# Moving two loads in a one-layer encoder kernel: the second gate weight tile in front of the first attention loads, and the attention mask into the opening

## The chip, the cores and the metric

The kernel runs on one NeuronCore of one Trainium2 chip. The metric is the device time of one execution in microseconds (us), lower is better. TensorE (PE in the profile, with its weight loads as PEld) does matrix products, VectorE (DVE) and ScalarE (ACT) do elementwise work, GpSimd (POOL) does a little arithmetic and issues DMAs, SyncE (SP) only issues DMAs. Each engine runs its own instructions in order; SP and POOL are also queues in which a DMA that has to wait holds up the DMAs behind it.

## The reference

One layer of a streaming encoder, for a prompt of 1024 tokens and a sample of 32 tokens with 512 cached ones, width 1024, all in float32. What matters here:

```python
ada = silu(c) @ w_ada + b_ada                      # six modulation vectors
h   = rms_norm(x, g_pre_mix) * (1 + sc1) + sh1
p   = h @ w_in                                     # columns: q latent 384 | kv latent 256 | rope key 32
                                                   #          | SB q 512 | SB k 512 | SB v 512 | gate A 1024 | gate B 1024
...
# branch B, stick-breaking attention, strictly causal
z    = (q_b @ k_b.T) * SB_SCALE
mask = kpos[None, :] < qpos[:, None]
sp   = where(mask, softplus(z), 0);  later = reverse_cumsum(sp) - sp
o_b  = where(mask, exp(log_sigmoid(z) - later), 0) @ v_b
...
merged = sigmoid(g_a) * (o_a @ w_proj_a) + sigmoid(g_b) * (o_b @ w_proj_b)
x = x + gt1 * rms_norm(merged @ w_out, g_post_mix)
# then a convolutional FFN and its residual
```

## The kernel before, in words

The stages run one after the other in one program: the opening (`stage_h`: modulation and the normed, transposed input), the projections to SB queries, keys and values (`stage_qkv`), stick-breaking attention (`stage_sb`), latent attention, merge, and the FFN. Products are made to float32 precision from a high and a low part of each operand: a raw weight tile of 128 x 1024 floats is loaded into a buffer `wr`, ACT writes its rounded high part `wh` (helper `hi`, L68) and DVE the rest `wl` (helper `lo`, L71), and three matmuls are accumulated (L75 to L77). There are two buffers each of `wr`, `wh` and `wl`.

**Opening.** `stage_h` loads four tiles of the prompt, the weights of the first half of the modulation (`ada_half(0)`), normalizes and transposes, loads the first `w_in` tiles, then the other four tiles and the second half.

**Projections.** `stage_qkv` makes most of the products two weight tiles at a time in `pair()` (five pairs; the last is q 2 and q 3). Each product has two column blocks `b`, and its banks in PSUM are copied out by ACT between products (L611, L619, L627, L636). Behind pair number 3 (the fourth) stands the load of the mask of the sample's attention, `k_mask[:, 128:]`, 128 x 272 floats, into a buffer `sg` by POOL, and its copy by ACT to `msk` in bfloat16 (L687, L688). `msk` is read much later, in `sb_sample` (stage_lat). After the last pair, gate tile 0 (columns 2208 to 2335 of `w_in`) is loaded and split.

**Stick-breaking.** `stage_sb` first loads queries, keys and values of head 0 (`queries(0, 0)`, six loads, and `values(0, 0)`), which the projections have spilled to DRAM. From then on every load of this stage goes through `load` (L83) with `issue_after(self.sent)`, so that SP issues them in the order in which they are written. Inside the stage the order on PE, ACT and DVE is written out by hand as a string `ORDER`, in which each letter is a step and what follows is the head's group, row block and half:

```python
S0.0 a0.0 f1 S0.1 f1 a0.1 e0.0 S1.0 f1 l0.0 f1 e0.1 f1 a1.0 l0.1 e1.0 f1 x0.0 c0.0 f1 d0.0 E0.0 f2 S2.0a
x0.1 c0.1 f1 l1.0 f1 a2.0a x1.0 d0.1 c1.0 W f1 e2.0a f1 G l2.0a w x2.0a f1 S1.1 f1 a1.1 f1 E0.1 f2 e1.1
```

`S` are scores (L1207, L1208: the second uses the keys' low part `KLz`, loaded from `kl`), `a e l x c d E` the elementwise chain on ACT and DVE (L747 to L767), `T h v V` turn the weights and multiply them by the values. The rest fills PE: `f` is one of the 24 steps (three blocks of 352 tokens, eight steps each) of the product of a gate tile, `G` copies a finished block from PSUM (ACT, L1129) and stores it, `W` and `w` split the next gate tile (ACT, DVE). The generator `gates` (L1096 on) makes these steps; at the first `f` of gate tile m it also loads the raw tile m + 1. Gate tile 1 is therefore written, and issued on SP, behind `queries(0, 0)` and `values(0, 0)`.

Outside such hand-ordered blocks the order on each engine is chosen at compile time by a scheduler with a cost model of its own, so a line can run well before or after its neighbours in the text. Pools of successive stages share memory (`reuse_waits="tile"`): a load into a new tile waits until the last reader of the old tiles under it has run.

Of the kernel before, what the change touches and what calls it, by code (L numbers as in the profile page):

```python
# [44 lines left out]
class K:  # L45
# [329 lines left out]
    def stage_h(self):  # L375
        nc = self.nc
        self.new_H()
        a = self.a
        self.Fq = self.tc.alloc_tile_pool(name="fq", bufs=1, reuse_waits="tile")
        self.fq = self.Fq.tile([P, KT, TP - 512 + TS], F32, name="fq")  # L380
        with self.tc.tile_pool(name="st_h", bufs=2, reuse_waits="tile") as tp, self.tc.tile_pool(name="wada", bufs=8, reuse_waits="tile") as wp:
            self.ada_prep(tp)
            xts = []

            def load(t):
                x = self.tl(wp, [P, D], F32, "x")
                nc.sync.dma_start(x, a["x_prompt"][0, t * P : (t + 1) * P])
                nc.vector.tensor_scalar(x, x, self.rstd(self.sumsq(x, P, tp, "jk0", 1024), D, P), None, ALU.mult)
                xts.append(x)

            def norm(t, hf):
                self.norm_T(t, xts[t : t + 4] if t < 8 else [xs], self.g1, 0, tp, 4 * hf, 4 * hf + 4)

            for t in range(4):
                load(t)
            self.ada_half(0, wp, tp)
            norm(0, 0)
            w = [self.w_in_tile(672)]
            for t in range(4, 8):
                load(t)  # L400
            w.append(self.w_in_tile(672 + 512))
            self.in_w = w
            norm(4, 0)
            xs = self.tl(tp, [P, 256], F32, "xs")
            self.quarters(xs, a["x_sample"][0], nc.gpsimd)
            nc.gpsimd.dma_start(self.sel, a["k_sel"])
            self.ada_half(1, wp, tp)
            nc.vector.tensor_scalar(xs, xs, self.rstd_s(xs, tp), None, ALU.mult)
            norm(0, 1)
            norm(8, 0)  # L410
            norm(4, 1)
            norm(8, 1)
# [30 lines left out]
    def stage_qkv(self):  # L443
# [232 lines left out]
        for i, (ta, tb) in enumerate(pairs):  # L676
            pair(i, ta, tb, *U[i % 2 * 2 : i % 2 * 2 + 2])
            if i == 0:
                with self.tc.issue_after(l2):
                    self.ada_bias(2)  # L680
            elif i == 1:
                late = self.late_loads(sg().bitcast(F32))
            elif i == 2:
                self.late_vectors(late)
            elif i == 3:
                mk = sg().bitcast(F32)[:, :272]
                nc.gpsimd.dma_start(mk, a["k_mask"][:, P:])  # L687
                nc.scalar.copy(self.msk, mk)  # L688
        self.in_w.append(self.w_in_tile(2208))
        for r, c in self.SB:  # L690
            nc.gpsimd.dma_start(self.sbd[r, c], self.sb[r, c])
# [357 lines left out]
    def sb_sample(self, b):  # L1049
# [43 lines left out]
            nc.gpsimd.dma_start(self.obd[k][:, TP:T], os[:, k])  # L1093
        yield

    def gates(self):  # L1096

        nc = self.nc
        v = lambda t: t.rearrange("p (k c) -> p k c", k=8)
        w, ps, ada = [self.w_in_tile(2208)], [], []  # L1100
        self.next_w = w
        raw = []

        def steps():
            for m in range(16):
                wh, wl = w.pop(0)
                for b, (c0, n) in enumerate(self.BLK):
                    if b == 0:
                        c = 2208 + (m + 1) * P if m < 15 else 3 * P
                        raw.append(self.wload([(0, 1024, self.a["w_in"][0, :, c : c + P].rearrange("(k p) c -> p k c", p=P), 8)]))  # L1110
                    ps.append((m, c0, n, self.bank("mm")))
                    for k in range(KT):
                        self.mm3(ps[-1][3][:, :n], wh[:, k], wl[:, k], self.Hh[k][:, c0 : c0 + n],
                                 self.Hl[k][:, c0 : c0 + n], k == 0, k == KT - 1)
                        if k < KT - 1:
                            yield
                    if b == 1 and self.ada_sum is not None:
                        ada.append(self.ada_turn())
                    yield

        step = steps()

        def do(kind):
            if kind == "f":
                next(step)
            elif kind == "G":
                m, c0, n, x = ps.pop(0)
                g = self.tl(self.At, [P, 512], F32, "nat", 3 if self.At is self.Sp else 2)
                nc.scalar.copy(g[:, :n], x[:, :n])  # L1129
                self.gsent = nc.gpsimd.dma_start(self.gd[m, :, c0 : c0 + n], g[:, :n]).ins  # L1130
            elif kind == "A":
                self.ada_step(4, self.sm2, self.Sp, ada)
                if not self.ada_todo:
                    self.sample_load(1)
            elif kind in "DQ":
                ada.pop(0)()
            elif kind == "W":
                w.append((self.tl(self.W, [P, 1024], F32R, "wh"), self.tl(self.W, [P, 1024], F32R, "wl")))
                self.hi(w[0][0], raw[0])
            else:  # L1140
                self.lo(w[0][1], raw.pop(0), w[0][0])
                w[0] = tuple(v(x) for x in w[0])

        return do
# [14 lines left out]
    def stage_sb(self):  # L1159
        nc = self.nc  # L1160
        self.att_rows()
        S = self.Sp = self.At = self.tc.alloc_tile_pool(name="sb", bufs=2, side="right", reuse_waits="tile")
        def place(*tags):
            for g, w, n in tags:
                for _ in range(n):
                    self.tl(S, [P, w], F32R if g[0] == "P" else F32, g, n)

        place(("o", 256, 2), ("PTh", 512, 2), ("PTl", 512, 2))
        self.KLz, Q, KH, V = [None] * 2, [None] * 2, [None] * 2, [None] * 2
        t = lambda n: self.tl(S, [P, TP], F32R, n, 1)  # L1170

        def values(p, h):
            if p:
                V[h] = t(f"V{h}")
            self.load(V[h].bitcast(F32).rearrange("r (t d) -> r t d", t=8), self.vd[p][:, :, h])

        def queries(p, h):
            r, o = slice(64 * h, 64 * h + 64), slice(64 - 64 * h, 128 - 64 * h)
            d = lambda x, n: self.load(x.bitcast(F32), self.spilt[n][p][r])
            if p:  # L1180
                Q[h], KH[h] = t(f"Q{h}"), t(f"KH{h}")
            d(Q[h][r], "qh")
            d(KH[h][r], "kh")
            d(KH[h][o], "kh")
            d(Q[h][o], "ql")
            d(self.KLz[h][r], "kl")
            d(self.KLz[h][o], "kl")

        V[1], self.KLz[1], Q[1], KH[1] = t("V1"), t("KL1"), t("Q1"), t("KH1")
        place(("ada", 256, 2), ("nat", 512, 3))  # L1190
        self.diagonals(S)
        for _ in range(3):
            self.tl(S, [P, TP], F32, "A")
        V[0], self.KLz[0], Q[0], KH[0] = t("V0"), t("KL0"), t("Q0"), t("KH0")
        self.sm2 = self.tc.alloc_tile_pool(name="att", bufs=2, reuse_waits="tile")
        for g, w, n in (("big", BIG, 3), ("A", TP, 2)):
            for _ in range(n):
                self.tl(self.sm2, [P, w], F32, g)

        self.sent = self.wlast  # L1200
        queries(0, 0)
        self.ada_w, self.ada_sum = [], None
        values(0, 0)

        def score(h, ps, i, c0, n):
            q = slice(i * P, (i + 1) * P)
            nc.tensor.matmul(ps[:, :n], Q[h][:, q], KH[h][:, c0 : c0 + n], start=True, stop=False)  # L1207
            nc.tensor.matmul(ps[:, :n], Q[h][:, q], self.KLz[h][:, c0 : c0 + n], start=False, stop=True)  # L1208

        fill = self.gates()  # L1210
        E = mybir.EngineType
        for p in range(4):
            then = {"S2.0a": lambda: queries(p, 1), "S2.1a": lambda: values(p, 1)}
            if p == 0:
                then["S2.1a"] = lambda: (values(p, 1), self.ada_fetch(4, self.sm2))
            if p < 3:
                then.update({"S3.1b": lambda: queries(p + 1, 0), "V3.0": lambda: values(p + 1, 0)})
            with self.tc.manual_schedule(engines={E.PE, E.Activation, E.DVE}):
                self.sb_attend(score, lambda b, h: V[h][:, b * P : b * P + P], self.store(self.obd[p]), fill, then)
        self.in_w.append(self.next_w.pop(0))  # L1220
        S.release()
        self.At = self.sm2
        self.sm3 = self.tc.alloc_tile_pool(name="att2", bufs=2, reuse_waits="tile")
# [1526 lines left out]
```

## Time and profile before

| | |
|---|---|
| median of 3 runs | 1679.88 us (1679.72 to 1681.83) |
| the profiled execution, its own time | 1686.64 us |
| its span, first to last instruction | 1684.8 us |
| PE busy | 98% |
| DVE, ACT, POOL busy | 75%, 60%, 18% |
| mean granted PE clock | 0.992 |
| DMA | 260.62 MB, mean 155 GB/s |

The profiled execution is 0.4% longer than the median of the runs. "Busy" is the share of the span in which an engine executes; a view of waits gives, for an engine and line, the line that ended its idle time, with the sum, the count and the longest. The granted clock is the share of full speed at which PE was allowed to run.

### The profile page before, as it was taken

The page shows a single profiled execution, that of the slowest core. Times are in us where ns is not written, and L with a number is a line of the kernel's source. Part 1 is how long each engine was busy: PE and PEld are TensorE (multiplying, and loading weights), DVE is VectorE, ACT ScalarE, POOL GpSimd, SP SyncE. Part 2 cuts the span into 40 slices and gives each one's busy share as a digit, 9 for nine tenths or more (in the row PEclk, how much of TensorE's full clock was granted, in tenths as well). Part 3 has the DMA queues.
Part 4 walks back from the last instruction along what each step waited for, and adds up shares of the span by engine and source line. Part 5 has one row for each costly group of instructions (what it writes and reads, how often), then busy time and mean ns, then how long its engine had stood idle before and what let it go on. Part 6 is the DMA issues. An engine that isn't in the chain of part 4 may idle for free. (4 is left out here: it accounts for less than half of the span.)

```text
span 1684.8 us, 30265 instructions
## 1 busy us (share of the span) xinstructions
PE 1643.0 (98%) x11592; PEld 1509.2 (90%) x11592; DVE 1268.4 (75%) x2139; ACT 1008.5 (60%) x1946; POOL 300.9 (18%) x581
## 2 busy tenths in 40 slices
PE   6999999999999999999999999999999999999996
PEld 3999999999999889988988799999999999877885
DVE  4865598989883588987766789878778778787455
ACT  4544587878884488987772675544444444454442
POOL 2113312111121221111000222211112111200013
PEclk8999999999999999999999999999999999999999
DMA  9345876566733443231374523333333333797643
GB/s 331 101 130 183 273 226 182 165 169 176 208 109 89 131 103 115 74 97 49 134 266 135 175 89 125 130 126 104 128 126 100 133 128 104 245 331 246 190 142 118
DMA packets 194145, 260.62 MB, mean 155 GB/s; under 512 B 23374, under 2 KB 132304, under 8 KB 193936
## 3 DMA queue, kind: packets, MB, share of 16 engines
q1 hardware_dynamic: 172944, 198.50, 38.0%
q0 software_dynamic: 20688, 59.56, 10.1%
q8 instruction: 91, 1.49, 0.4%
q10 hardware_dynamic: 368, 0.63, 0.1%
q14 instruction: 54, 0.44, 0.1%
HBM read 191.11 MB, written 67.82 MB: 154 GB/s over the span
## 5 line engine op out<-in xcount | busy, mean ns | idle before, releaser
L68 ACT ACTIVATE wh<-wr 128x1024 fp32r<-128x1024 f32 (+2 forms) x151 | 130.1, 863 | 226.8 <-PE s L2204 85.8
L71 DVE TENSOR_TENSOR wl<-wr,wh 128x1024 fp32r<-128x1024 f32 (+2 forms) x151 | 148.2, 984 | 87.1 <-ACT wh L68 86.9
L75 PE MATMUL mm<-hh,wh 128*128 128x352 f32 x456 | 153.4, 336 | 2.8 <-ACT nat L1129 2.8
L76 PE MATMUL mm<-hl,wh 128*128 128x352 f32 x456 | 149.5, 328 | 0.4 <-DVE hl L333 0.4
L77 PE MATMUL mm<-hh,wl 128*128 128x352 f32 x456 | 149.0, 327 | 0.0
L2203 PE MATMUL mm<-T,wh 128*128 128x256 f32 (+1 forms) x376 | 108.2, 288 | 2.0 <-ACT q L627 2.0
L2205 PE MATMUL mm<-T,wl 128*128 128x256 f32 (+1 forms) x376 | 107.1, 285 | 0.4 <-DVE wl L71 0.2
L2204 PE MATMUL mm<-T,wh 128*128 128x256 f32 (+1 forms) x376 | 106.6, 284 | 0.0
L2205 PE MATMUL s<-T,wl 128*128 128x256 f32 (+1 forms) x348 | 99.3, 285 | 0.0
L2203 PE MATMUL s<-T,wh 128*128 128x256 f32 (+1 forms) x348 | 99.2, 285 | 0.0
L2204 PE MATMUL s<-T,wh 128*128 128x256 f32 (+1 forms) x348 | 98.8, 284 | 0.0
L71 DVE TENSOR_TENSOR wl<-S,wh 128x1024 fp32r<-128x1024 f32 (+1 forms) x55 | 59.2, 1077 | 51.7 <-ACT wh L68 51.3
L75 PEld LDWEIGHTS mm<-hh,wh 128*128 128x128 f32 x456 | 86.9, 191 | 6.4 <-ACT nat L1129 3.1
L76 PEld LDWEIGHTS mm<-hl,wh 128*128 128x128 f32 x456 | 87.1, 191 | 3.4 <-DVE hl L333 1.7
L2344 DVE SCALAR_TENSOR_TENSOR u<-u,c,u 128x1058 f32<-128x1058 f32 x68 | 87.0, 1317 | 2.0 <-ACT u L2341 0.7
L808 PE MATMUL tr<-c,A 128*128 128x128 f32 x576 | 87.1, 272 | 0.0
L77 PEld LDWEIGHTS mm<-hh,wl 128*128 128x128 f32 x456 | 86.9, 191 | 0.2
L68 ACT ACTIVATE wh<-S 128x1024 fp32r<-128x1024 f32 (+1 forms) x55 | 51.8, 943 | 47.6 <-PE s L2204 13.4
L2205 PE MATMUL tr<-T,wl 128*128 128x272 f32 (+1 forms) x272 | 77.7, 286 | 0.2 <-DVE wl L71 0.2
L2203 PE MATMUL tr<-T,wh 128*128 128x272 f32 (+1 forms) x272 | 77.8, 286 | 0.0
L2204 PE MATMUL tr<-T,wh 128*128 128x272 f32 (+1 forms) x272 | 77.3, 284 | 0.0
L2334 POOL COPY c<-u 128x2 f32<-128x2 f32 x44 | 26.7, 607 | 265.3 <-DVE u L2280 229.4
(770 smaller groups left out, 5836.8 us busy)
## 6 DMA issues: line engine op xcount, KB each, us to landing
wr<-in_w_up_dram SPq DMA_DIRECT2D x44, 512.0 KB, 4.1
dr<-in_w_down_dram SPq DMA_DIRECT2D x43, 512.0 KB, 5.3
wr<-in_w_in_dram SPq DMA_DIRECT2D x33, 512.0 KB, 6.7
A<-in_w_ada_dram SPq DMA_DIRECT2D x32, 512.0 KB, 5.8
wr<-gdn SPq DMA_DIRECT2D x30, 512.0 KB, 4.2
gdn<-u POOLq DMA_DIRECT2D x23, 512.0 KB, 5.2
gd<-nat POOLq DMA_DIRECT2D x48, 176.0 KB, 3.5
t<-gd SPq DMA_DIRECT2D x16, 528.0 KB, 4.7
```

What stands on the lines that cost most here:

```text
L68: self.nc.scalar.activation(out, in_, AF.Identity, scale=scale)
L71: return self.nc.vector.tensor_tensor(out, full, hi.bitcast(F32), ALU.subtract)
L75: m(ps, lh, rh, start=start, stop=False)
L76: m(ps, lh, rl, start=False, stop=False)
L77: self.pe = m(ps, ll, rh, start=False, stop=stop).ins
L808: self.nc.tensor.transpose(tr[:, (2 * s + q) * P : (2 * s + q + 1) * P], at[q][:, b * P : b * P + P], self.idt)
L2203: m(ps[:, :n], w[0][:, k], x[0][:, k, c], start=first and k == 0, stop=False, skip_group_check=True)
L2204: m(ps[:, :n], w[0][:, k], x[1][:, k, c], start=False, stop=False, skip_group_check=True)
L2205: i = m(ps[:, :n], w[1][:, k], x[0][:, k, c], start=False, stop=k == 3, skip_group_check=True)
L2334: nc.gpsimd.tensor_copy(self.CV[:, 0:2, cc], u[:, 1024:1026])
L2344: nc.vector.scalar_tensor_tensor(y, u[:, w : w + YW], self.cvT[:, w, cc : cc + 1], y, ALU.mult, ALU.add)
```

## The change

Gate tile 1 is no longer loaded by the first `f` step but by `stage_sb` itself, directly in front of `queries(0, 0)`; the other gate tiles are loaded where they were. The mask is loaded in `stage_h` into a small tile of its own, between the first `w_in` tile and the other half of the prompt, again by a DMA of POOL, and turned to bfloat16 by DVE instead of ACT.

```diff
@@ stage_h
             norm(0, 0)
             w = [self.w_in_tile(672)]
+            mk = self.tl(tp, [P, 272], F32, "mk")
+            nc.gpsimd.dma_start(mk, a["k_mask"][:, P:])
+            nc.vector.tensor_copy(self.msk, mk)
             for t in range(4, 8):
                 load(t)
@@ stage_qkv
                 self.late_vectors(late)
-            elif i == 3:
-                mk = sg().bitcast(F32)[:, :272]
-                nc.gpsimd.dma_start(mk, a["k_mask"][:, P:])
-                nc.scalar.copy(self.msk, mk)
         self.in_w.append(self.w_in_tile(2208))
@@ gates
+    def gate_raw(self, m):
+        c = 2208 + m * P if m < 16 else 3 * P
+        return self.wload([(0, 1024, self.a["w_in"][0, :, c : c + P].rearrange("(k p) c -> p k c", p=P), 8)])
+
     def gates(self):
...
-        raw = []
+        raw = [self.ahead]
...
                     if b == 0:
-                        c = 2208 + (m + 1) * P if m < 15 else 3 * P
-                        raw.append(self.wload([(0, 1024, self.a["w_in"][0, :, c : c + P].rearrange("(k p) c -> p k c", p=P), 8)]))
+                        if m:
+                            raw.append(self.gate_raw(m + 1))
@@ stage_sb
+        self.ahead = self.gate_raw(1)
         self.sent = self.wlast
         queries(0, 0)
```

## The prediction

> **What bounds the kernel now.** I read the page first, for the engine that sets the pace.
>
> ```profile
> PE 1643.0 (98%) x11592; PEld 1509.2 (90%) x11592; DVE 1268.4 (75%) x2139; ACT 1008.5 (60%) x1946; POOL 300.9 (18%) x581
> ```
>
> TensorE (PE) is busy in 98% of the span, so an edit elsewhere gains only where it closes a hole in PE or keeps PE's clock up. The second view is the list of waits, for PE alone, from 150 to 400 us, the stretch that holds both edited places; this is its whole answer:
>
> ```profile
> PE mm L75 <- ACT nat L1129: 2.8, 1, 2.8
> PE mm L2203 <- ACT q L627: 2.0, 1, 2.0
> ```
>
> Two holes, 2.8 and 2.0 us, both ended by ScalarE (ACT). The third view is ACT's timeline at both places (start, duration, engine and line; in brackets the idle time before it and what ended that):
>
> ```profile
> 161.57 0.37 ACT L627 COPY q<-mm 128x256 f32<-128x256 f32 x1 [1.16 <-PE mm L2205]
> 165.63 0.42 ACT L688 CAST c<-sg 128x272 bf16<-128x272 f32 x1 [3.69 <-DMA sg<-in_k_mask_dram]
> 165.96 0.62 ACT L68 ACTIVATE wh<-wr 128x512 fp32r<-128x512 f32 x1
> 166.49 0.37 ACT L627 COPY q<-mm 128x272 f32<-128x272 f32 x1
> ...
> 200.06 0.44 ACT L747 ACTIVATE A<-s 128x320 f32<-128x320 f32 x1 [0.88 <-PE s L1208]
> 204.89 1.06 ACT L68 ACTIVATE wh<-wr 128x1024 fp32r<-128x1024 f32 x1 [4.39 <-DMA wr<-in_w_in_dram]
> 205.85 0.45 ACT L749 ACTIVATE A<-A 128x320 f32<-128x320 f32 x1
> 206.21 0.43 ACT L1129 COPY nat<-mm 128x352 f32<-128x352 f32 x1
> ```
>
> At 161.94 ACT stops for 3.69 us at the mask's copy, whose load has not landed; queued behind it is the copy of a PSUM bank that PE must overwrite next. At 200.50 it stops for 4.39 us at the split of gate tile 1 (step W), whose raw tile has not landed; behind it is the evacuation (step G) of the bank that the third block of gate tile 0 needs. The change moves exactly these two loads. PE's timeline and the 2-us windows (busy PE, weight loads, DVE, ACT, POOL, then granted PE clock, DMA share, GB/s) show what each hole costs:
>
> ```profile
> 164.61 0.28 PE L2205 MATMUL mm<-T,wl 128*128 128x256 f32 x1
> 166.91 0.40 PE L2203 MATMUL mm<-T,wh 128*128 128x272 f32 x1 [2.02 <-ACT q L627]
> ...
> 203.39 0.33 PE L76 MATMUL mm<-hl,wh 128*128 128x352 f32 x1
> 203.55 0.32 PE L77 MATMUL mm<-hh,wl 128*128 128x352 f32 x1
> 206.69 0.66 PE L75 MATMUL mm<-hh,wh 128*128 128x352 f32 x1 [2.82 <-ACT nat L1129]
> 209.50 0.47 PE L1207 MATMUL s<-KH,Q 128*128 128x320 f32 x1
> ```
>
> ```profile
> 166.00:168.00 2.00, 1.09 (x8) 1.09 (x9) 1.39 (x3) 2.00 (x6) 0.37 (x1) 1.00 0.00 0
> 206.00:208.00 2.00, 1.31 (x4) 1.31 (x5) 2.00 (x4) 2.00 (x6) 0.57 (x1) 0.62 0.96 313
> 208.00:210.00 2.00, 2.00 (x9) 1.99 (x9) 1.75 (x5) 1.29 (x3) 0.38 (x1) 0.53 0.84 300
> ```
>
> The first hole leaves the clock at 1.00. After the second it is 0.62 and 0.53 for two windows, so that hole costs more than its length.
>
> **Part 1, the mask leaves the projections.** ACT no longer waits at 161.94, and L627 can follow as soon as its product is done, some 3 us earlier than 166.49. PE's 2.02 us come back: **-2.0**. Nothing else is late there: PE has no other wait in this stretch, by the list above. The load's issue on GpSimd's queue (POOL) goes too, and nobody waited for that queue.
>
> **Part 2, gate tile 1 in front.** SyncE's queue (SP) now, the landing of this tile (min/median/max of the one load), and the split of the buffer that it is loaded into:
>
> ```profile
> 181.28 0.54 SPq L83 DMA_DIRECT2D Q<-qh  x1
> 183.95 1.57 SPq L83 DMA_DIRECT2D KL<-kl  x2
> 185.63 1.14 SPq L83 DMA_DIRECT2D V<-vd  x1
> 186.87 1.94 SPq L83 DMA_DIRECT2D wr<-in_w_in_dram  x1
> ...
> DMA to landing us min/median/max: 18.0/18.0/18.0
> ...
> 178.60 1.29 DVE L71 TENSOR_TENSOR wl<-wr,wh 128x512 fp32r<-128x512 f32 x2
> ...
> wr<-in_w_in_dram SPq DMA_DIRECT2D x1, 512.0 KB, 3.8
> ```
>
> Now the tile is issued at 186.87, behind six loads of queries and keys and one of values, and lands 18.0 us later, at 204.9: ACT's wait. There are two raw buffers; the one it gets is last read by the splits that end at 178.60 + 1.29 = 179.89. In front, it can be issued there, and SP is free again before 181.28, when the queries' own buffers become free, so their issue is not delayed. Landing: an equal tile, issued near 175 on quiet queues, took 3.8 us (the last row); at twice that it is there by 188, 12 us ahead of step W. Then W (1.06) and L749 (0.45) run from 200.50 and G near 201.9 instead of 206.21; PE wants it at 203.87. The hole closes: **-2.8**. The slow clock goes with it. Matmuls of 352 columns start 0.16 us apart at full clock (203.39 to 203.55); nine took 209.50 - 206.69 = 2.81 us instead of 1.44, a loss of 1.4, and the clock column gives the same (1.31 x 0.38 + 2.00 x 0.47 = 1.4). With the scores just behind, **-1.5**. ACT was held 4.39 us and PE 2.82 + 1.5, so neither gains a backlog on the other, and what is late next is PE's own work.
>
> [...]
>
> The cost is the place in front of the keys. The equal tile in 1-us windows (same columns), the gap in which the new one would start, the keys' landing, and the matmuls that use them:
>
> ```profile
> 176.00:177.00 1.00, 1.00 (x11) 1.00 (x10) 0.37 (x1) 0.00 (x0) 0.00 (x0) 1.00 0.80 183
> 177.00:178.00 1.00, 1.00 (x11) 1.00 (x10) 0.05 (x1) 0.06 (x1) 0.00 (x0) 1.00 1.06 321
> 180.00:181.00 1.00, 1.00 (x11) 1.00 (x10) 0.93 (x2) 0.28 (x1) 0.65 (x1) 1.00 0.07 16
> 182.00:183.00 1.00, 1.00 (x11) 1.00 (x10) 0.45 (x2) 0.48 (x1) 0.23 (x1) 1.00 0.94 205
> ...
> DMA to landing us min/median/max: 8.5/8.8/9.0
> ...
> 194.34 0.37 PE L1207 MATMUL s<-KH,Q 128*128 128x256 f32 x1
> 194.54 0.28 PE L1208 MATMUL s<-KL,Q 128*128 128x256 f32 x1
> ```
>
> The tile takes about 0.80 + 1.06, say 2.0 us, of all 16 DMA engines. Issued at 179.9 it begins about a microsecond later, as the equal tile did, so it finds little of the gap at 180 to 181; from 182 on the engines are full. I take 0.6 us as hidden and 1.4 us as pushed onto the keys, 2.4 at worst, since stores from POOL share the engines. The second load of kl is issued near 184.7 and lands 8.5 to 9.0 us later, at about 193.5; PE needs it at 194.54. Slack 1.0, so S0.0 waits 0.4 to 1.4 us, and 0 if the tile hides better. PE runs in order, so nothing covers it. I take **+1.0**, by the larger of the two delays, as the engines are above 0.9 busy right behind. That is under the 2.02 us that left the clock alone. The values are used only after the first weights are turned. The tile also no longer sits between these loads and those of head 1, which start no later for it.
>
> **Part 3, the mask in the opening.** There the DMA engines are full, and PE waits for what they bring:
>
> ```profile
> 16.00:17.00 1.00, 1.00 (x13) 0.46 (x16) 0.00 (x0) 0.00 (x0) 0.00 (x0) 1.00 1.04 383
> 21.22 0.42 DVE L293 COPY ada<-s 128x256 f32<-128x256 f32 x1 [6.23 <-PE s L291]
> 24.50 0.76 DVE L332 CAST hh<-hf 128x512 fp32r<-128x512 f32 x2
> 22.26 1.06 ACT L68 ACTIVATE wh<-wr 128x1024 fp32r<-128x1024 f32 x1 [11.45 <-DMA wr<-in_w_in_dram]
> 26.00:27.00 1.00, 1.00 (x4) 1.00 (x5) 0.45 (x1) 1.00 (x3) 0.92 (x2) 0.50 1.01 359
> ```
>
> 128 x 272 floats are 139 KB: at 383 GB/s 0.36 us, and everything behind it lands that much later, the weights before the first modulation and the w_in tile for which ACT waits until 22.26: **+0.4**. The cast on DVE costs 0.3 to 0.5 us (two of 512 columns take 0.76, ACT's took 0.42); DVE is idle for 6.23 us ahead of 21.22, which hides it, and also a wait of several us for the load, which on ACT was 3.69. If it stood behind 24.5, where DVE is busy and PE follows it, it would cost those 0.5. Its issue on POOL goes ahead of work with time to spare, since DVE and ACT both wait for DMAs and products here. The new small tile moves other tiles' addresses; no row prices that, I take 0, within ±0.5.
>
> **Sum** against the profiled execution: -2.0 - 2.8 - 1.5 + 1.0 + 0.4 = -4.9 us, from 1686.64 to 1681.7. The median of the runs is 1679.88, 6.8 below that execution; I carry the difference over: **1675.0**. Bounds of the unknown costs: keys 0 to 2.4 - 1.0 = 1.4, opening 0.2 (half of the transfer) to 0.9 (all of it and the cast), so -6.1 to -4.0; with ±0.5 for the addresses, 1673.3 to 1676.4. What a measurement of this kernel can tell from no change is about 0.2%, 3.4 us.
>
> **The rivals.**
> 1. *The clock does not come back.* The dip moves to another hole (the new wait at S0.0, or the opening, where the clock is at 0.50 at 26 us), or is not there in timed runs. Then only holes count: -2.0 - 2.8 + 1.4 = -3.4, 1676.5. Against it stand the windows at 206 and 208. [...]
> 2. *The tile was late only in the profiled execution.* It lands at 204.9 behind full queues, and the timed runs are 6.8 us shorter; were it 3 us sooner there, L1129 would be ready near 203.2 and there is no hole to close. What is left is the mask: -2.0 + 1.4 = -0.6, 1679.3. Against it: 6.8 us in 1680 is 0.4%, which does not take 3 us from 18.
> 3. *SP is blocked in front of the queries (slower).* If ACT's order in the last pair changes, because the mask's copy is gone, and the split of that raw buffer runs only just before its product, near 187, then the tile waits there and all queries and keys stand behind it on SP. Issued at 187.5 instead of 181.28 they land 6.2 us later; PE waits 6.2 - 1.0 = 5.2 us at S0.0, plus 1.4 from the tile's own transfer and 1.5 of slow clock: 8.1 - 6.3 + 0.4 = +2.2, 1682.1. It decides once the split is about 5 us later than now. For it: the order on ACT is the scheduler's and not the text's (L688 is written behind the pair between whose two L627 it runs), so taking it out can move others. Against it: the two splits of that buffer run as one pair at 178.60, well before they are needed.
> 4. *The opening costs more* than the one transfer: the mask's cast or a changed order there puts PE back by 2 more: -2.9, 1677.0.
>
> **How the numbers follow.** Forecast 0.58; rival 1 0.13; rival 2 0.09; rival 3 0.13; rival 4 0.07. Faster by over 0.2%: the forecast and about half of rival 1 (0.64). Within: the other half, rivals 2 and 4 (0.23). Slower: rival 3 (0.13). The range goes from 1673.2, the forecast's low end, to 1679.8, which takes in rivals 1, 2 and 4; rival 3 and some 0.05 below are left out.
>
> **What would show it.** Right: ACT without a DMA wait at L627 and at the split of gate tile 1; no PE wait for L1129 near 200; clock 1.00 from 200 to 210; a wait of about 1 us at L1207 or L1208 at the start of stick-breaking; the first L75 of the opening 0.4 us later. Wrong: the queries' first load issued later relative to the last pair than now, a hole over 2.8 us at S0.0, or a new DVE wait for the mask with PE behind it.

## The result and the profile after

| | before | after |
|---|---|---|
| median | 1679.95 us (20 runs, 1677.52 to 1683.88) | 1677.24 us (20 runs, 1674.71 to 1680.79) |
| ratio of the times | 1 | 0.9985 [0.9978, 0.9992] |
| the profiled execution, its own time | 1686.64 us | 1675.33 us |
| its span | 1684.8 us | 1673.5 us |
| mean granted PE clock | 0.992 | 0.994 |

The change makes the kernel about 2.5 us faster (1.3 to 3.7 by the interval): really faster, but by less than the 0.2% that the prediction took as its bound. The forecast was 1675.0, a gain of 4.9; the measured time lies inside the stated range of 1673.2 to 1679.8, but the gain is about half the forecast. The two profiled executions differ by 11.3 us, over four times what the runs differ by. Both numbers are right, and most of what follows is about why.

The page of after. Against the page of before, PE is busy for 6.9 us less with the same 11592 matmuls, and ACT has one instruction less and DVE one more, the mask's copy:

```profile
PE 1636.1 (98%) x11592; PEld 1505.2 (90%) x11592; DVE 1268.7 (76%) x2140; ACT 1007.4 (60%) x1945; POOL 297.8 (18%) x581
```

The list of waits of PE from 150 to 400 us, which held two rows of 2.8 and 2.0 us before, holds none after. ACT's timeline at the same two places (L630 is before's L627, L1132 its L1129, the splits are still L68):

```profile
160.08 0.37 ACT L630 COPY q<-mm 128x256 f32<-128x256 f32 x1 [1.16 <-PE mm L2209]
161.46 0.63 ACT L68 ACTIVATE wh<-wr 128x512 fp32r<-128x512 f32 x1 [1.01 <-PE mm L2208]
161.99 0.37 ACT L630 COPY q<-mm 128x272 f32<-128x272 f32 x1
...
196.60 1.05 ACT L68 ACTIVATE wh<-wr 128x1024 fp32r<-128x1024 f32 x1
197.55 0.46 ACT L748 ACTIVATE A<-A 128x320 f32<-128x320 f32 x1
197.91 0.44 ACT L1132 COPY nat<-mm 128x352 f32<-128x352 f32 x1
```

The two evacuations L630 now stand 1.9 us apart (160.08 and 161.99) instead of 4.9, and the split of gate tile 1 starts at 196.60 with nothing waited for. The clock behind it stays at 1.00, by the 2-us windows of after:

```profile
200.00:202.00 2.00, 2.00 (x16) 2.00 (x15) 1.23 (x3) 1.71 (x5) 0.47 (x2) 1.00 1.04 424
202.00:204.00 2.00, 2.00 (x15) 2.00 (x14) 1.82 (x4) 1.94 (x6) 0.42 (x1) 1.00 0.96 338
```

SP's timeline of after, then the landing of kl (median us, last number) and the first scores. The gate tile is the second of the two `wr` loads in the first row, and the queries' load follows a microsecond behind it:

```profile
171.04 5.46 SPq L83 DMA_DIRECT2D wr<-in_w_in_dram  x2
177.49 1.19 SPq L83 DMA_DIRECT2D Q<-qh  x1
...
181.06 1.59 SPq L83 DMA_DIRECT2D KL<-kl  x2
...
KL<-kl SPq DMA_DIRECT2D x2, 256.0 KB, 8.2
...
190.55 0.37 PE L1211 MATMUL s<-KH,Q 128*128 128x256 f32 x1
190.75 0.29 PE L1212 MATMUL s<-KL,Q 128*128 128x256 f32 x1
```

The keys land in 8.2 us (8.8 before), and the first scores wait for nothing. Last, the opening in DVE's timeline of after: the mask's cast, and the two ends of the modulation's halves:

```profile
6.99 0.30 DVE L401 CAST c<-mk 128x272 bf16<-128x272 f32 x1 [4.83 <-DMA mk<-in_k_mask_dram]
21.58 0.42 DVE L293 COPY ada<-s 128x256 f32<-128x256 f32 x1 [6.24 <-PE s L291]
43.89 0.42 DVE L293 COPY ada<-s 128x256 f32<-128x256 f32 x1 [3.00 <-PE s L291]
```

### The profile page after: what moved, and what is told of

Same layout as the page of the kernel before. It is cut to its first block, busy times and chain, and to the rows that moved or that the text cites. A ratio compares the mean times of both kernels' runs of the same rounds, so it can differ in the third digit from the quotient of the medians.

```text
span 1673.5 us, 30264 instructions
## 1 busy us (share of the span) xinstructions
PE 1636.1 (98%) x11592; PEld 1505.2 (90%) x11592; DVE 1268.7 (76%) x2140; ACT 1007.4 (60%) x1945; POOL 297.8 (18%) x581
## 5 line engine op out<-in xcount | busy, mean ns | idle before, releaser
L68 ACT ACTIVATE wh<-wr 128x1024 fp32r<-128x1024 f32 (+2 forms) x151 | 130.1, 864 | 226.6 <-PE s L2208 86.6
L807 PE MATMUL tr<-c,A 128*128 128x128 f32 x576 | 87.2, 272 | 0.0
L68 ACT ACTIVATE wh<-S 128x1024 fp32r<-128x1024 f32 (+1 forms) x55 | 51.8, 943 | 47.6 <-PE s L2208 13.0
```

The lines of the kernel that those rows point to most:

```text
L68: self.nc.scalar.activation(out, in_, AF.Identity, scale=scale)
L807: self.nc.tensor.transpose(tr[:, (2 * s + q) * P : (2 * s + q + 1) * P], at[q][:, b * P : b * P + P], self.idt)
```

## The experiments

The times of one batch were measured beside the kernel before on the same chip: 1679.60 us for the first four, 1680.32 for the next four.

### The two parts alone, and before once more

`e0` is the kernel before, unchanged. `e1` has the gate part of the change and leaves the mask where it was; `e2` has the mask part alone:

```diff
e1_gate_only, against before            e2_mask_only, against before
+    def gate_raw(self, m): ...         +            mk = self.tl(tp, [P, 272], F32, "mk")
...                                     +            nc.gpsimd.dma_start(mk, a["k_mask"][:, P:])
-        raw = []                       +            nc.vector.tensor_copy(self.msk, mk)
+        raw = [self.ahead]             ...
...                                     -            elif i == 3:
+                        if m:          -                ...
...
+        self.ahead = self.gate_raw(1)
```

> The kernel before, unchanged, as a second profile and a measure of the noise: ratio 1.000. Theory A (both holes and the slow clock behind the second are there in every execution): the profile again shows waits of PE of about 2.0 us at L627 and 2.8 us at L1129 and a clock of 0.5 to 0.6 behind the second. Theory B (the slow clock is a matter of the execution): both holes, but the clock behind the second is 1.00 in this profile, or its length differs. Theory C (the second hole belongs to the one profiled execution): the wait for L1129 is under 1 us or gone.

> The change without its mask part: gate tile 1 in front, the mask loaded and copied by ScalarE in the projections as before. Theory A: -4.3 us (2.8 of hole, 1.5 of clock), ratio 0.9974. Theory B: -2.8 us on average, ratio 0.9983. Theory C: between 0 and -1 us, ratio above 0.9994. In the profile: the 2.0 us wait at L627 stays, no wait for the gate bank's copy, no wait at the first scores.

> The change without its gate part: the mask loaded and cast in the opening, gate tile 1 loaded where it was. By the sum of the prediction -2.0 + 0.4 = -1.6 us, ratio 0.9990, in all three theories. If the opening pays more than its transfer (rival 4): 0 to -0.5 us. In the profile: no wait at L627, the 2.8 us wait at L1129 stays, the opening 0.3 to 0.4 us later.

| | median | against before |
|---|---|---|
| e0, before again | 1678.55 | 0.9996 [0.9987, 1.0004] |
| e1, gate part | 1679.03 | 0.9996 [0.9987, 1.0005] |
| e2, mask part | 1677.64 | 0.9986 [0.9977, 0.9994] |

By these ratios the mask part alone carries -2.4 us, the gate part -0.7 with an interval that holds zero: as far from no change as the unchanged kernel was. On top of the mask part it adds nothing that these runs can tell, 0.9985 for both parts against 0.9986 for the mask alone. The list of waits of PE from 150 to 400 us in e0 and in e1 has this one row each (a different line number for the same matmul):

```profile
PE mm L2203 <- ACT q L627: 2.1, 1, 2.1
```

```profile
PE mm L2208 <- ACT q L627: 1.8, 1, 1.8
```

In e0 the gate tile is still in its old place, and yet the hole of 2.8 us is not there. ACT's timeline at the split, and the tile's row among the DMA issues (KB, us to landing):

```profile
198.57 1.05 ACT L68 ACTIVATE wh<-wr 128x1024 fp32r<-128x1024 f32 x1
...
wr<-in_w_in_dram SPq DMA_DIRECT2D x1, 512.0 KB, 11.1
```

The tile landed in 11.1 us instead of 18.0, and the split waited for nothing. In e2, the tile again in its old place, the hole was expected to stay at 2.8 us, and it was between the two; ACT's row, the issue, and PE's only row of waits:

```profile
200.48 1.06 ACT L68 ACTIVATE wh<-wr 128x1024 fp32r<-128x1024 f32 x1 [2.19 <-DMA wr<-in_w_in_dram]
...
wr<-in_w_in_dram SPq DMA_DIRECT2D x1, 512.0 KB, 15.4
...
PE mm L75 <- ACT nat L1128: 0.6, 1, 0.6
```

So the hole is real, and its size is drawn anew in each execution.

### The mask neither in the opening nor in the way

`e3` has the gate part, and loads the mask by POOL into a tile of its own, behind the first spills, long before ACT's copy at its old place:

```diff
+            self.sp = nc.gpsimd.dma_start(self.spilt[n][p], fl(x)).ins
...
+        mk = A.tile([P, 272], F32, name="mk")
+        with self.tc.issue_after(self.sp):
+            nc.gpsimd.dma_start(mk, a["k_mask"][:, P:])
...
-                mk = sg().bitcast(F32)[:, :272]
-                nc.gpsimd.dma_start(mk, a["k_mask"][:, P:])
```

> Gate tile 1 in front as in the change, and the mask loaded into a buffer of its own behind the first spills, where the DMA engines are idle (53 to 61 us in the profile of before), and copied by ScalarE at its old place, long after it has landed. If the opening's 0.4 us is a real price: 0.4 us below the changed kernel, so -2.7 - 0.4 = -3.1 us from before by the measured time, ratio 0.9981. If the opening pays nothing: same as the changed kernel, 0.9985.

1676.97 us, 0.9984 [0.9975, 0.9993]: the same as the change, within what these runs can tell. The list of waits from 150 to 400 us has no row. The first modulation ends at 21.17, against 21.58 in after (rows of DVE's L293), so the +0.4 of the opening belongs to the mask's load. The time doesn't show it: in e3's trace the 0.4 us is lost again before the first scores, which come 147.1 us after the end of the opening (43.49 to 190.63) where after takes 146.7; why is not known.

### The same transfer in three places

A load of 512 KB that nobody reads, written as below, was put in front of gate tile 1 in before (`e4`), behind gate tile 1 and the queries to values in after (`e5`), and between gate tile 1 and the queries in after (`e6`):

```diff
+        dm = self.dr.tile([8, P, P], F32, name="dm")
+        self.load(dm, self.a["w_in"][0, :, 0:P].rearrange("(k p) c -> k p c", p=P))
```

> The kernel before with one more load of 512 KB (a copy of a weight block into unused DRAM) on SyncE's queue right in front of gate tile 1, which so lands later. The profiles so far show the tile landing 18.0, 11.1 and 15.4 us after its issue, and a hole only where it is not there by the split (step W). Theory C (the hole is a matter of how late the tile lands, and most executions just escape it): now nearly every execution has it, several us long and with the slow clock behind it: +4 to +8 us from before. Theory D (the tile's lateness costs little even where it occurs, since PE has other work): within 1 us of before.

> The changed kernel with the same extra load at the same place in the queue, which is now behind gate tile 1. Theory C: the same time as the changed kernel, -2 to -3 us from before, and 6 to 10 us below the kernel before with the extra load. If the extra load costs by itself (head 1's loads, the spills): that many us above the changed kernel.

> The changed kernel with a further load of 512 KB between gate tile 1 and the first queries: twice the traffic in front of the keys. In the changed kernel the keys land about 1 us before the first scores, as in the kernel before, so the one tile in front has cost them nothing. By the prediction's price (1.4 to 2.4 us of delay for each tile): a wait of PE of 0.4 to 1.4 us at the first scores, +1 us on the changed kernel. If the engines still have room there: no wait, same time as the changed kernel.

| | median | against before |
|---|---|---|
| e4, in front of the tile, old place | 1686.93 | 1.0043 [1.0026, 1.0060] |
| e5, behind the tile, new place | 1677.05 | 0.9983 [0.9975, 0.9992] |
| e6, between tile and queries | 1679.41 | 0.9996 [0.9985, 1.0006] |

e4 makes the mechanism as large as one likes. Its waits (of PE, then of ACT), and its 2-us windows:

```profile
PE mm L75 <- ACT nat L1129: 4.8, 1, 4.8
...
ACT wh L68 <- DMA wr<-in_w_in_dram: 6.3, 1, 6.3
```

```profile
206.00:208.00 2.00, 0.00 (x0) 0.00 (x0) 0.00 (x0) 0.00 (x0) 0.00 (x0) 1.00 1.05 421
208.00:210.00 2.00, 0.00 (x0) 0.00 (x0) 0.69 (x1) 1.78 (x4) 0.00 (x0) 0.82 1.07 303
210.00:212.00 2.00, 1.98 (x7) 1.98 (x8) 2.00 (x4) 1.97 (x5) 0.56 (x1) 0.50 1.03 230
212.00:214.00 2.00, 2.00 (x10) 1.96 (x8) 1.37 (x4) 1.05 (x3) 0.54 (x1) 0.50 1.13 204
```

ACT is held 6.3 us, PE 4.8, and the clock falls to 0.50 behind it. From the first scores to the first turned weights (L1207 to L808) e4 takes 17.6 us (195.72 to 213.36) where e0 takes 11.1: 6.5 us more, and the time against before is 6.6 us more by the medians, 7.2 (4.4 to 10.1) by the ratio. One execution stands here beside a median of six, so that the two agree this closely is partly luck. The same load behind the tile costs nothing. In e5's windows behind the split (which starts at 198.09) PE is full, at clock 1.00, though the DMA engines are as full as in e4:

```profile
200.00:202.00 2.00, 2.00 (x13) 1.91 (x13) 2.00 (x4) 1.56 (x4) 0.57 (x1) 1.00 1.04 422
202.00:204.00 2.00, 2.00 (x16) 2.00 (x15) 1.20 (x4) 1.71 (x5) 0.54 (x1) 1.00 1.01 412
```

e6 prices what the prediction feared of the new place, at twice the traffic: kl lands in 9.9 us, and the second score waits for it. The rows of the landing and of PE's timeline:

```profile
KL<-kl SPq DMA_DIRECT2D x2, 256.0 KB, 9.9
...
193.75 0.36 PE L1214 MATMUL s<-KL,Q 128*128 128x256 f32 x1 [0.92 <-DMA KL<-kl]
```

That is 0.9 us of waiting, and a time 2.4 us over e5, which has the same load in another place (the intervals of the two overlap, and the trace accounts for only a part of it). One tile in front is hidden, a second one is not.

### Eight masks in the opening

`e7` copies the mask seven more times in the opening, to DRAM, so that only the transfer is multiplied:

```diff
+            dm = self.dr.tile([7, P, 272], F32, name="dm")
+            for i in range(7):
+                nc.gpsimd.dma_start(dm[i], a["k_mask"][:, P:])
```

> The changed kernel with seven more copies of the mask's 139 KB on GpSimd's queue in the opening (into unused DRAM). By the prediction's price of 0.36 us each, the weights land 2.5 us later and the kernel is 2.5 us above the changed kernel, about the same as before. If PE's slow clock in the opening sets its end and not the transfers: 0 to +1 us on the changed kernel.

1680.97 us, 1.0007 [0.9998, 1.0016]: 3.9 over e5 in the same batch. DVE's timeline of e7:

```profile
23.95 0.42 DVE L293 COPY ada<-s 128x256 f32<-128x256 f32 x1 [7.06 <-PE s L291]
46.15 0.42 DVE L293 COPY ada<-s 128x256 f32<-128x256 f32 x1 [3.01 <-PE s L291]
```

The first modulation is 23.95 - 21.58 = 2.37 us later than in after, 0.34 us for each copy: the price of 139 KB in a full stretch, as the prediction had worked it out (0.36). The second modulation is later by about as much, 46.15 - 43.89 = 2.26. The time rose by 1.5 us more than that; the intervals of e5 and e7 leave room for it, and it is not explained. In this one profile the last stage, from the first product of L2546 (1445.0 us) to the end of the span, takes 234.4 us where after takes 230.9 (its L2543, from 1442.6), far from the edit.

### Before, three more times

To see how often the hole is there, the unchanged kernel before was profiled three more times.

> The kernel before, unchanged, for one more profiled execution of it. Theory (the landing of gate tile 1 in its old place varies from one execution to the next): it lands 11 to 18 us after its issue, ACT waits 0 to 4.4 us at its split and PE's hole for L1129 is 0 to 2.8 us, below 1 us more often than not, since the gate part alone moved the time by 0.6 us. Rival (the hole of 2.8 us is the usual one, and the execution without it was the exception): landing near 18 us, hole 2 to 3 us. In both, the mask's wait of 1.5 to 2.2 us at L627 is there.

> As the run before it, a further execution of the kernel before. Theory: a landing between 11 and 18 us and a hole between 0 and 2.8 us, not the same as in the run before it. Rival: landing near 18 us and a hole of 2 to 3 us again. In both, the mask's wait of 1.5 to 2.2 us at L627.

> As the two runs before it, a further execution of the kernel before. Theory: a landing between 11 and 18 us and a hole between 0 and 2.8 us. Rival: landing near 18 us and a hole of 2 to 3 us. In both, the mask's wait of 1.5 to 2.2 us at L627.

Their times are 1679.17, 1681.19 and 1679.85 us. ACT's row for the split and the tile's issue, for e8, e9 and e10:

```profile
201.09 1.06 ACT L68 ACTIVATE wh<-wr 128x1024 fp32r<-128x1024 f32 x1 [0.61 <-DMA wr<-in_w_in_dram]
...
wr<-in_w_in_dram SPq DMA_DIRECT2D x1, 512.0 KB, 15.0
```

```profile
202.31 1.06 ACT L68 ACTIVATE wh<-wr 128x1024 fp32r<-128x1024 f32 x1 [0.84 <-DMA wr<-in_w_in_dram]
...
wr<-in_w_in_dram SPq DMA_DIRECT2D x1, 512.0 KB, 14.8
```

```profile
200.00 1.05 ACT L68 ACTIVATE wh<-wr 128x1024 fp32r<-128x1024 f32 x1
...
wr<-in_w_in_dram SPq DMA_DIRECT2D x1, 512.0 KB, 13.0
```

All seven executions with the tile in its old place, by landing (e2 and e4 are other kernels; e4's tile was issued behind the extra load, so only its waits compare):

| execution | landing | ACT's wait | PE's hole | L1207 to L808 |
|---|---|---|---|---|
| e0 | 11.1 | 0 | 0 | 11.1 |
| e10 | 13.0 | 0 | 0 | 11.1 |
| e9 | 14.8 | 0.84 | 0 | 11.1 |
| e8 | 15.0 | 0.61 | 0 | 11.1 |
| the one the prediction read | 18.0 | 4.39 | 2.82 | 15.6 |
| e2 | 15.4 | 2.19 | 0.6 | 12.0 |
| e4 | | 6.34 | 4.8 | 17.6 |

The last column runs from the first matmul of L1207 (194.34 in the execution that the prediction read, 190.55 in after, where the line is L1211) to the first of L808 (L807 in after). The later row in these two:

```profile
209.97 0.49 PE L808 MATMUL tr<-c,A 128*128 128x128 f32 x3
```

```profile
201.65 0.49 PE L807 MATMUL tr<-c,A 128*128 128x128 f32 x3
```

One rule fits all of them: PE's hole is ACT's wait less 1.6 us, or nothing. And the landing decides: the split is due 13 to 14.5 us after the tile's issue. Of five executions of before, one had this hole. Their mean of the stage is (4 x 11.1 + 15.6) / 5 = 12.0, so that removing the hole is worth some 0.9 us on the average, which is inside the interval of e1 (-2.2 to +0.8). One in five is a rough figure, and rather too high: the execution with the hole, 1686.64 us, is longer than every timed run of before (at most 1684.52). The theory of the expectations stands, and its rival falls. The mask's wait was there in all three, 2.1 us, as both had it. (e9 was also expected to differ from e8, and hardly does.) SP and POOL issue the same transfers in the same order in these executions; what it is that makes the same load land after 11 us in one execution and after 18 in another is open; it was not tried.

## Why the prediction was right, and where it was not

**Part 1, the mask out of the projections, -2.0: right, and a little small.** From the end of the opening to the first scores, before takes 148.9 us (45.49, below, to 194.34), and so do e0 and e8; e9 takes 149.0. With the mask out, after takes 146.7 (43.89 to 190.55) and e2 146.6.

```profile
45.49 0.42 DVE L293 COPY ada<-s 128x256 f32<-128x256 f32 x1 [3.00 <-PE s L291]
```

That is -2.2, in place and size, and unlike the other hole this one was there in every execution with the mask in its old place (1.8 to 2.1). What the prediction missed is that the clock can fall behind it too. In e10 this stage takes 150.5 us, with the same hole of 2.1; its 2-us windows:

```profile
166.00:168.00 2.00, 2.00 (x14) 2.00 (x13) 1.20 (x3) 0.82 (x3) 0.53 (x1) 0.63 0.44 131
168.00:170.00 2.00, 2.00 (x11) 2.00 (x11) 0.98 (x1) 0.39 (x1) 1.30 (x2) 0.51 0.00 0
```

e4 shows the same, 0.58 and 0.56, and 150.3 us; the other five with this hole stay at 1.00. The mean of the five executions of before is 149.2, so the mask is worth -2.6 on the average.

**Part 2, gate tile 1 in front, -2.8 and -1.5: the mechanism right, the size wrong.** This is the step that failed. Late tile, held ACT, late evacuation, hole, slow clock: each link is there and e4 drives it to 6.5 us. In the profiled execution the stage gives back 15.6 - 11.1 = 4.5, near the 4.3 of the sum. But the sum took 4.3 from one execution for all of them, where the mean of five is 0.9 and e1 measured 0.7. The prediction even carried the difference of that execution to the median (6.8 us) over as a constant, when part of it was the hole itself. Rival 2 had said this, at 0.09, and was argued away by scaling: 6.8 us of 1680 is 0.4%, which does not take 3 us from 18. A landing isn't stretched with the whole; the same load took 11.1 to 18.0 us while the times moved by a few tenths of a per cent.

**The keys, +1.0 (0 to 1.4): nothing.** It came out at its low end. Behind the tile the keys take no longer to land: by the median of the two loads of kl, 7.8 to 8.4 us in four executions with the tile in front (after, e1, e3, e5), 7.4 to 8.8 in the five of before. SP only gets to the second load of kl later, 4.0 to 4.4 us after the queries' first load instead of 3.2 to 3.6. By issue and longest landing it is there at the latest 12.2 to 12.7 us after the queries' first load, where before had 11.1 to 12.6; the second score needs it at 13.3. The tile thus costs about half a microsecond of slack, less than the 1.4 that the prediction took, and the execution that it read had the least slack of the five. The price exists, but begins with the second tile (0.9 us of waiting in e6).

**Part 3, the opening, +0.4: right** in the trace (21.22 to 21.58, and 0.34 for each further copy), and the cast on DVE is hidden, though not in the idle time where the prediction put it: it runs at 6.99, 0.30 us, behind a wait of 4.83 for its load, which holds up small DVE steps (L143 starts at 7.20, in before at 4.85). They have caught up by the copy of L218, at 9.35 (9.41 in before), and PE's first product of the modulation waits for its weights, until 11.42 (11.07 in before).

**The sum as measured:** -2.6 for the mask and -0.9 for the hole, both on the average with their clock, 0 for the keys, +0.4 for the opening: -3.1, inside the measured -2.5 (-3.7 to -1.3). With the two mis-sized terms put right (0.9 in place of 4.3, 0 in place of 1.0) the prediction's own sum would have been -2.5, or 1677.4; as it was, it came out 2.2 us low. The case that came true is rival 2 with the keys hidden, rather than the forecast: a gain just inside the 0.2%, though a larger one than the 0.6 us that rival 2 had left over. That 1677.24 lies in the stated range is owed to the rivals that the range takes in; the sum's own bounds, 1673.3 to 1676.4, do not hold it. Rival 1 doubted the slow clock, but kept the hole of 2.82 us in front of it, and four of the five executions of before have neither. Rival 3 (SP blocked) falls: the queries' first load is issued 13.06 us ahead of the first scores in both profiles (181.28 to 194.34, 177.49 to 190.55). Rival 4's figure, 1677.0, is the nearest to the measured time, by luck: the opening cost 0.4 us, and no wait in the trace bears out 2 more.

**The 11.3 us between the two profiled executions** are then 2.2 of the mask, 4.5 of the hole and its clock, 1.6 of the opening (last section), and some 3 us spread over stages that the change doesn't touch. Only the first is the change's in every execution.

## What to carry to other kernels

A wait read from one profiled execution is one draw: before it goes into a sum, ask whether its releaser is a transfer behind busy queues, whose landing varies (gate tile 1 here: 11.1 to 18.0 us), or one that is late in every execution (the mask here: a hole of 1.8 to 2.1 us each time), and weigh the first kind by how often it is late. When the profiled execution lies clearly above the median of the runs, suspect that the hole you want to close is part of the difference. Loading a tile ahead of a crowd can still pay as insurance, as the same extra load behind it (no cost) and in front of it (6.6 us) shows; in this kernel as it stands, by e1, it brought nothing that the runs can tell.

## What the runs showed of the hardware

**The opening has two lengths or more, with the same instructions.** The opening's PE clock is granted differently from one execution to the next. The 2-us windows from 34 to 36 us in before, and in e0, the same kernel:

```profile
34.00:36.00 2.00, 1.68 (x13) 1.03 (x5) 0.69 (x1) 2.00 (x4) 0.00 (x0) 0.50 1.04 386
```

```profile
34.00:36.00 2.00, 1.42 (x21) 0.73 (x13) 0.69 (x1) 2.00 (x4) 0.00 (x0) 1.00 1.05 387
```

At 0.50 PE gets through 13 matmuls, at 1.00 through 21. The second modulation ends, by DVE's timelines, at 45.49 in before but here in e9 and e10, also the kernel before:

```profile
46.34 0.43 DVE L293 COPY ada<-s 128x256 f32<-128x256 f32 x1 [3.10 <-PE s L291]
```

```profile
43.44 0.42 DVE L293 COPY ada<-s 128x256 f32<-128x256 f32 x1 [2.99 <-PE s L291]
```

That is a spread of 2.9 us, more than the change itself is worth, and part of why single executions differ by as much as they do. What sets the clock that the opening is granted was not tried.

**The same hole drops the clock in one execution and not in another.** After the hole of 1.8 to 2.1 us in the projections the clock stayed at 1.00 in five executions and fell to 0.5 to 0.6 for two windows in two (e10, e4), which cost 1.6 and 1.4 us (150.5 and 150.3 us of that stage against 148.9). It fell after 2.82 us (0.62 and 0.53) and after 4.8 us (0.50 in the windows above), and not after 0.92 us at e6's scores. So the prediction's reading, that 2.02 us leave the clock alone and 2.82 do not, was drawn from one case of each. What decides whether the clock falls after such a hole was not tried.
